# Gated attention as two streams, local attention divided at the gates, one rank for both; scan level 2 issued together with level 4

## The chip, the cores and the metric

The kernel runs on one core of one Trainium2 chip. The metric is the time of one execution in device microseconds; less is better. A core has a matrix engine (TensorE, PE in the profile), with its weight loads listed apart as PEld, a vector engine (VectorE, DVE), an activation engine (ScalarE, ACT), a general engine (GpSimd, POOL) and SyncE (SP), which here issues all DMAs. Each engine works off its own instructions in order and waits on semaphores for the others.

## What is computed

A trunk of two layers over two requests of 2048 and 512 tokens, 2560 rows of width 1024 together, in float32. The even layer projects the rows once and feeds two branches: gated linear attention (GLA, four heads, one scan in each direction with a decay that depends on the data) and local softmax attention (SWA, eight query heads over two key heads, a window of 128 to each side). Each branch is multiplied by its own gate, both go through one output projection. The odd layer is a gated convolution. A layer norm follows each.

```python
def gla_mixer(q, k, v, z, gdown, ...):
    logd_f = heads(log_sigmoid(gd_f @ w_up_f + b_f) / GLA_TAU)      # and logd_b
    o_f = _gla_scan(qh, kh, vh, logd_f, strict=False)
    o_b = flip(_gla_scan(flip(qh), flip(kh), flip(vh), flip(logd_b), strict=True))
    o = (o_f + o_b) * rsqrt(mean(square(o_f + o_b)) + NORM_EPS) * norm_g
    return o * silu(z)

def swa_mixer(q, k, v, z, rel_bias, sink):
    s = where(mask, einsum('bnqkgd,bnskd->bnkgqs', qh, kb) + bias, -inf)
    m = maximum(max(s, -1), sk)
    e = exp(s - m)
    p = e / (sum(e, -1) + exp(sk - m))
    o = einsum('bnkgqs,bnskd->bnqkgd', p, vb)
    return o * silu(z)

def trunk(x, ...):
    for l in range(DEPTH):
        sub = even_sublayer(x, ...) if l % 2 == 0 else odd_sublayer(x, ...)
        x = layer_norm(DN_ALPHA * x + sub, ln_g[l], ln_b[l])
```

## The kernel before

The rows are cut into five groups of 512 (group 4 is the short request) and twenty chunks of 128. The dense products run group by group in the order of the list `stages` in `run`: for groups 4, 3, 2, 1 the token-major part of the input projection ("tok") and the channel-major part ("ch"), then the output projection of group 4, the input projection of group 0, the odd layer's input of group 4, and so on through output projections and the odd layer, where groups are taken in pairs. Each float32 operand is split into a rounded high part and a low rest, and a product is three matrix instructions into one PSUM tile: high x high, high x low, low x high. A weight of 128 x 1024 is loaded into a raw tile `ws` (two buffers), ACT rounds it into `wh` (three buffers), and POOL subtracts to get `wl` (two buffers), in `cook` and `cook_low`; `dense_ch` then runs 16 instructions with `wh` and 8 with `wl` into an `acc` tile. The operands are `st` tiles.

Attention is threaded between these dense instructions. The order is made when the program is built: `Flow` holds generators ("side" work), `Model` keeps a clock for each engine with costs of its own, and after every dense step `pump` lets a generator continue whose inputs are due by the model's clock. Generators with a lower rank come first; the residual and operand streams have rank 0, `gla_stream` has rank 1, `swa_front` and `swa_back` rank 2. A generator that yields a list of tiles waits until the model has them written. The engines then run that order, with real semaphores. `defer` puts off a step until its tiles are due.

GLA. `gla_stream` goes through the chunks from the last to the first. For each it loads q and the decays (`gla_load`, tiles `qn`, `tA`), k in two copies (`gla_load_k`, `KK`), and runs `inside`: Q gets the decays multiplied in (`QQ`), and then seven levels s = 1, 2, 4, ..., 64 follow. A level multiplies blocks of the scaled K and Q against each other on PE (the helper `blocks`, 16 instructions of 32 x 32, which the trace lists as 32 records), then scales K and Q on DVE to the next level. For s up to 16 ACT makes a copy `km` of half of K. Level 8 is not issued at its turn: its half of Q is copied into a tile `qm` of the `md` tag, and its blocks go out together with those of level 16. Behind the levels, still in `inside`, K is transposed on PE (`turn`), the output product, the backward state `S` and the product for the forward scan are made. When a request is through, `along` carries the forward state over its chunks and makes the normed, gated output in `mix_s`.

SWA. `swa_front` takes a chunk and a key head at a time: Q·K into `ps` tiles, bias and maximum on DVE into `P`, the exponential with its sum `den` on ACT, the reciprocal, and four multiplications of `P` by it on DVE. `swa_back` transposes `P` on PE, splits it into `pth` and `ptl`, multiplies with V, and, once both key heads are there, POOL multiplies the output `o` by the gate `gb`, which goes to `mix_s`.

Tiles: PSUM has four `acc` and four `ps` tiles. In SBUF the tag `md` has eight tiles of 128 x 512, most of them for one dense output on its way to DRAM; the tag `y` has four of 128 x 1024.

Everything is issued by one helper, so that all lines of the profile read L242; groups are told apart by their tiles. DMAs are all issued by SP, one after the other.

Of the kernel before, what the change touches and what calls it, by code (L numbers as in the profile page):

```python
# [10 lines left out]
F32 = mybir.dt.float32  # L11
# [3 lines left out]
ALU = mybir.AluOpType  # L15
# [247 lines left out]
class Flow:  # L263
# [32 lines left out]
    def flush(self, everything=False, name=None):  # L296
        now, keep = [], []
        for one in self.late:
            (now if everything or name in one[2] or (name is None and one[0] <= self.t) else keep).append(one)
        self.late = self.model.late = keep  # L300
        for one in now:
            one[1]()

# [73 lines left out]
class Trunk:  # L377
    def __init__(self, tc, nc, I, y_out, ctx):
# [22 lines left out]
        self.kb_s = dr("kb_s", (2, 128, 2, T))  # L401
        self.vb_s = dr("vb_s", (NC, 128, 256))
        self.qf_s = dr("qf_s", (NC, 128, 512))
        self.up_s = dr("up_s", (128, 2, 512))
# [8 lines left out]
        self.bst = None  # L413
        self.blocks = []
        self.x, self.owned, self.refs, self.pairs, self.wblocks = {}, {}, {}, {}, {}
# [153 lines left out]
    def dense_ch(self, xh, xl, w=None, last=True):  # L569

        nc = self.nc
        wh, wl = w or self.weight()
        p = self.pd()
        for k in range(8):
            c = slice(k * 128, k * 128 + 128)
            nc.tensor.matmul(p[:], wh[:, c], xh(k), start=(k == 0), stop=False)
            nc.tensor.matmul(p[:], wh[:, c], xl(k), start=False, stop=False)
            yield
        if last:
            self.drop(wh)  # L580
            self.cook()
        for k in range(8):
            c = slice(k * 128, k * 128 + 128)
            nc.tensor.matmul(p[:], wl[:, c], xh(k), start=False, stop=(k == 7))
            if k % 2 and k < 7:
                yield
        if last:
            self.drop(wl)
        return p

# [85 lines left out]
    def setup(self):  # L676
        nc, c = self.nc, self.const
        nc.scalar.preload_act_table_set("natural_log_exp_and_others")
        load = self.load
        self.ident = load("ident", (128, 128))  # L680
        self.hl = load("hl", (128, 2))
        self.norm_g = load("norm_g", (128, 1))
        self.eps = c.tile([128, 2], F32, name="eps")
        nc.vector.memset(self.eps[:, 0:1], LN_EPS)
        nc.vector.memset(self.eps[:, 1:2], NORM_EPS)
        self.dtot = c.tile([128, NC, 4], F32, name="dtot")
        self.one = c.tile([128, 1], F32, name="one")
        nc.vector.memset(self.one[:], 1.0)
# [483 lines left out]
    def gla_load(self, c):  # L1172
# [5 lines left out]
        return q, T1  # L1178

    def gla_load_k(self, c):  # L1180
        K = self.e((128, 2, 512), "KK")
        for i in range(2):
            self.nc.sync.dma_start(K[:, i], self.k_s[c])
        return K

    def inside(self, c, first, last, ld, K, ahead):

        nc = self.nc
        q, T1 = ld
        Q = self.e((128, 2, 512), "QQ")  # L1190
        T2 = self.e((128, 2, 256), "tB")
# [28 lines left out]
        def grow_k(s):  # L1220
# [12 lines left out]
        Sb = self.bst if not last else None  # L1233
        wait = []
        for li, s in enumerate((1, 2, 4, 8, 16, 32, 64)):
            n = 512 // s
            pls = []
            if s in (8,):
                qm = self.m2(hold=True)
                nc.scalar.copy(qm[:].rearrange("p (b two s) -> p b two s", two=2, s=s), halves(Q, s))  # L1240
                wait.append((li, s, qm))
            else:
# [14 lines left out]
                for lt, t, qm in wait:  # L1257
                    km = kms.pop(t)
                    pls.append((lt, one(len(pls))))
                    blocks(pls[-1][1], lambda o: mk(km, o, [[1, 32]]), lambda o: qm[:, o:o + 32])  # L1260
                    self.drop(qm)
                wait = []
# [13 lines left out]
                else:  # L1276
                    for h in range(4):
                        for b in range(64 // s):
# [6 lines left out]
                                             tile_position=(0, hi))  # L1285
                kms.pop(s, None)
            km = None
# [12 lines left out]

            if s not in (8,):
# [6 lines left out]
            if s in (8,):  # L1308
# [6 lines left out]
            if s == 4:  # L1315
                v = self.e((128, 512), "v")
                nc.sync.dma_start(v[:], self.v_s[c])
# [5 lines left out]
        nc.vector.tensor_copy(self.dtot[:, c], mk(end, 4, [[1, 4]]))  # L1323
        ahead(0)
        self.flow.defer(lambda: nc.sync.dma_start(self.qf_s[c], Q[:, 1]), Q)

        def turn(i):
            pt = self.pw((128, 4, 128))
            for h in range(4):
                nc.tensor.transpose(pt[:, h], K[:, i, h * 128:h * 128 + 128], self.ident[:])  # L1330
            t = self.e((128, 4, 128), "km", bufs=2)
            nc.scalar.copy(t[:], pt[:])
            return t

        def grow(t):
            pv = self.pw((128, 4, 128))
            for h in range(4):
                nc.tensor.matmul(pv[:, h], t[:, h], v[:, h * 128:h * 128 + 128], start=True, stop=True)
            return pv

        kf = kb = None
        if not last:
            yield from self.bank()
            kf = turn(0)
# [3 lines left out]
                                  self.lmask16[:].rearrange("p (b s) -> p b s", s=32).unsqueeze(1).broadcast_to(wide),  # L1348
                                  acmp[:].unsqueeze(2).broadcast_to(wide))
        if not first:  # L1350
            yield from self.bank()
            kb = turn(1)
        ahead(1)
        yield [A, v] + ([Sb] if Sb is not None else [])
# [9 lines left out]
        if not first:  # L1364
# [6 lines left out]
            else:  # L1371
                for h in range(4):
                    nc.vector.scalar_tensor_tensor(Sn[:, h], Sb[:, h], mk(end, h, [[1, 1]]), pv[:, h],
                                                   op0=ALU.mult, op1=ALU.add)
            self.bst = Sn
        if not last:
# [4 lines left out]
            self.flow.defer(lambda: nc.sync.dma_start(self.m_s[c], A[:].rearrange("p h t -> p (h t)")), A)  # L1381
        yield [Q]

# [18 lines left out]
    def along(self, c, first, last, ld, ahead):  # L1402
# [13 lines left out]
        if not last:  # L1416
# [4 lines left out]
            else:  # L1421
                for h in range(4):
                    nc.vector.scalar_tensor_tensor(Sn[:, h], Sf[:, h], self.dtot[:, c, h:h + 1], m[:, h],
                                                   op0=ALU.mult, op1=ALU.add)
# [26 lines left out]
    def seq(self, g):  # L1451
        return (0, 16) if g < 4 else (16, 20)

    def gla_stream(self):
        for g in (4, 3, 2, 1, 0):
            yield "gla_in%d" % g
            c0, c1 = self.seq(g)
            ends = lambda c: (c == c0, c == c1 - 1)
            cs = list(range(4 * g + 3, 4 * g - 1, -1))
            ld, K = self.gla_load(cs[0]), self.gla_load_k(cs[0])  # L1460
            nxt = {}
            for i, c in enumerate(cs):
                yield [*ld, K]

                def ahead(n):
                    if i < 3:
                        nxt[n] = (self.gla_load, self.gla_load_k)[n](cs[i + 1])
                yield from self.inside(c, *ends(c), ld, K, ahead)
                ld, K = nxt.get(0), nxt.get(1)
            if 4 * g > c0:  # L1470
                continue
            self.bst = None
            ld = K = None
            nxt.clear()
            yield "done_e1_%d" % g
# [34 lines left out]
    def swa_front(self):  # L1510
# [16 lines left out]
        while left:  # L1527
# [10 lines left out]
            for kv in range(2):  # L1538
                while len(self.blocks) >= 2:
                    yield 1.0  # L1540
                hs = slice(4 * kv, 4 * kv + 4)
                Pt = self.e((128, 4, 385), "P", bufs=4)
                mx = self.sm((128, 4), "mx")
# [35 lines left out]
    def swa_back(self):  # L1579
# [17 lines left out]
        for n in range(40):  # L1597
# [20 lines left out]
            for kb in range(nk):  # L1618
# [14 lines left out]
                yield []  # L1633
            yield [pl, V]
            Pt = None
            self.blocks.pop(0)
# [466 lines left out]
    def run(self):  # L2103
# [101 lines left out]
```

## Time and profile before

| what | value |
|---|---|
| median of 3 runs | 2370.76 us (2369.61 to 2370.84) |
| profiled execution, its own time | 2370.12 us |
| its span, first to last instruction | 2368.1 us |
| granted PE clock, mean | 0.998 |
| DMA, mean over the span | 185 GB/s |
| PE waits, longest | 6.4 us, for the first `st` |

Busy times by engine over the span, in 40 slices (a digit is the busy share in tenths):

```profile
PE   8999999999999999999999999999999999999998
PEld 8888889888988888888888888878888877888887
DVE  2267756767767677577776467876566587656567
ACT  4666776656576645665577532543334343333431
POOL 5454435443444444444444467898887689988674
```

A row of the page gives the line, engine, operation, the tile written and the tiles read, partitions x elements and type, and the count. Then follow the busy time in us, the mean of one in ns, the idle time of the engine just before, and what ended it. PE's busy time is the union of instructions that overlap, so a 512-wide instruction is listed with some 395 ns though one starts about every 228.

### The profile page before, as it was taken

To read this page: it belongs to the slowest core of one execution; us is meant where nothing else is said; L and a number is where in the kernel's file an instruction comes from. 1 tells how busy PE (TensorE), PEld (TensorE's weight loads), DVE (VectorE), ACT (ScalarE), POOL (GpSimd) and SP (SyncE) were. 2 spreads that over 40 slices of the span, in tenths; PEclk is the share of its full clock that TensorE was granted. 3 is DMA by queue.
4 is the path that set the end of the run, shared out by engine and by line. 5 is a ranking of instruction groups with operands and counts; after the bars stand their busy time and mean duration, and the time that the engine had idled before them with its cause. 6 is when DMAs were issued, how large, how long until landed. Compare 5 with 4: busy or idle time off the path is not lost.

```text
span 2368.1 us, 43087 instructions
## 1 busy us (share of the span) xinstructions
PE 2343.9 (99%) x15830; PEld 1951.8 (82%) x15830; DVE 1582.8 (67%) x2699; ACT 1226.1 (52%) x2363; POOL 1418.4 (60%) x1610
## 2 busy tenths in 40 slices
PE   8999999999999999999999999999999999999998
PEld 8888889888988888888888888878888877888887
DVE  2267756767767677577776467876566587656567
ACT  4666776656576645665577532543334343333431
POOL 5454435443444444444444467898887689988674
PEclk9999999999999999999999999999999999999999
DMA  7977686676667657675478777232124633221573
GB/s 230 295 226 233 221 269 229 209 221 221 218 194 236 223 173 242 197 218 161 158 245 268 266 261 243 92 116 89 52 78 140 217 105 103 73 72 58 175 242 121
DMA packets 275057, 437.37 MB, mean 185 GB/s; under 512 B 21360, under 2 KB 160240, under 8 KB 274848
## 3 DMA queue, kind: packets, MB, share of 16 engines
q1 hardware_dynamic: 274848, 434.64, 56.5%
q8 instruction: 125, 2.05, 0.4%
q14 instruction: 84, 0.69, 0.1%
HBM read 319.72 MB, written 114.84 MB: 184 GB/s over the span
## 4 chain that ended last, share of the span: by engine, by line
PE 87%; DVE 5%; POOL 4%; DMA 2%; issue 1%; ACT 1%; SPq 0%; POOLq 0%; DVEq 0%; ACTq 0%
PE acc L242 71%; PE ps L242 17%; POOL wl L242 1%; POOL wh L242 1%; DVE st L242 1%; DVE bst L242 1%; DVE y L242 1%; POOL md L242 0%; SPq L242 0%; DVE QQ L242 0%; DVE P L242 0%; DVE KK L242 0%; DMA K<-kb_s 0%; DMA mix_s<-gb 0%; DMA op_s<-QQ 0%
## 5 line engine op out<-in xcount | busy, mean ns | idle before, releaser
L242 POOL TENSOR_TENSOR wl<-ws,wh 128x256 fp32r<-128x256 f32 (+1 forms) x912 | 750.7, 855 | 711.4 <-PE acc L242 478.0
L242 PE MATMUL acc<-st,wh 128*128 128x512 f32 x3160 | 828.5, 395 | 2.8 <-DVE pr L242 2.0
L242 PEld LDWEIGHTS acc<-st,wh 128*128 128x128 f32 x3160 | 580.9, 188 | 121.0 <-issue 3.1
L242 PE MATMUL acc<-st,wl 128*128 128x512 f32 x1744 | 471.9, 395 | 2.8 <-POOL wl L242 1.9
L242 PE MATMUL acc<-wh,st 128*128 128x512 f32 (+1 forms) x1680 | 389.4, 371 | 7.9 <-ACT st L242 6.4
L242 PEld LDWEIGHTS acc<-st,wl 128*128 128x128 f32 x1744 | 320.8, 188 | 68.0 <-POOL wl L242 4.1
L242 PEld LDWEIGHTS acc<-wh,st 128*128 128x128 f32 x1680 | 300.2, 189 | 55.1 <-ACT st L242 6.4
L242 ACT CAST wh<-ws 128x1024 fp32r<-128x1024 f32 (+2 forms) x252 | 249.0, 989 | 184.2 <-DMA ws<-in_w_oo 55.9
L242 PE MATMUL acc<-wl,st 128*128 128x512 f32 (+1 forms) x840 | 209.0, 368 | 0.6 <-POOL wl L242 0.5
L242 ACT ACTIVATE md<-md 128x512 f32<-128x512 f32 x264 | 164.7, 631 | 20.5 <-DVE md L242 14.9
L242 PEld LDWEIGHTS acc<-wl,st 128*128 128x128 f32 x840 | 150.7, 188 | 23.8 <-POOL wl L242 1.3
L242 DVE SCALAR_TENSOR_TENSOR md<-acc,md 128x512 f32<-128x512 f32 (+1 forms) x113 | 77.0, 683 | 81.5 <-ACT md L242 76.5
L242 DVE TENSOR_TENSOR st<-pr,st 128x512 fp32r<-128x512 f32 x115 | 98.5, 874 | 41.6 <-ACT st L242 41.2
L242 ACT ACTIVATE md<-acc 128x512 f32<-128x512 f32 (+1 forms) x133 | 76.2, 597 | 67.0 <-PE acc L242 66.5
L242 POOL TENSOR_TENSOR wh<-md,wh 128x256 fp32r<-128x256 f32 x118 | 96.7, 842 | 13.6 <-ACT wh L242 13.1
L242 ACT CAST pth<-ps 128x512 fp32r<-128x512 f32 x112 | 65.3, 583 | 73.1 <-PE ps L242 72.3
L242 DVE CUSTOM_DVE_ANT_0 P<-ps,P 128x384 f32<-128x384 f32 (+1 forms) x160 | 79.3, 525 | 29.6 <-PE ps L242 29.0
L242 ACT ACTIVATE P<-P,nm 128x385 f32<-128x385 f32 (+1 forms) x160 | 93.2, 587 | 3.9 <-DVE nm L242 3.9
L242 ACT ACTIVATE mv<-mv,eps 128x1 f32<-128x1 f32 x40 | 11.8, 295 | 151.8 <-DVE mv L242 147.7
L242 PE MATMUL acc<-P,wh 128*128 128x512 f32 x312 | 89.5, 400 | 0.4 <-POOL wh L242 0.4
L242 ACT COPY km<-KK 128x512 f32<-128x512 f32 x80 | 50.8, 635 | 72.2 <-DVE KK L242 50.9
L242 ACT CAST st<-pr 128x512 fp32r<-128x512 f32 x115 | 68.3, 617 | 30.3 <-DMA pr<-mix_s 12.9
(490 smaller groups left out, 4090.2 us busy)
## 6 DMA issues: line engine op xcount, KB each, us to landing
ws<-in_w_ch SPq DMA_DIRECT2D x105, 512.0 KB, 4.4
ws<-in_w_od SPq DMA_DIRECT2D x58, 512.0 KB, 4.2
ws<-in_w_oe SPq DMA_DIRECT2D x40, 512.0 KB, 3.8
ws<-in_w_oo SPq DMA_DIRECT2D x36, 512.0 KB, 3.5
K<-kb_s SPq DMA_DIRECT2D x32, 384.0 KB, 6.3
d_s<-md SPq DMA_DIRECT2D x40, 256.0 KB, 4.2
qb_s<-md SPq DMA_DIRECT2D x80, 128.0 KB, 3.9
tA<-d_s SPq DMA_DIRECT2D x20, 512.0 KB, 5.7
```

The costliest lines, as they stand in the source:

```text
L242: r = f(*a, **k)
```

## The change

The change has five parts.

1. Level 2 is treated like level 8: its half of Q is copied into an `md` tile, and its blocks go out with those of level 4.
2. `inside` ends after the levels. It puts what it has into a list `heads`, and a second generator, `gla_behind`, takes it from there: transposes of K, output product, state and forward product (the new function `behind`). The levels of the next chunk may run meanwhile; a counter `open` lets at most two chunks be between. Copies of K (`km`) and the transposed K (`turn`) come from the `md` tag as well, and `KK` and `QQ` may take `y` tiles.
3. `P` is no longer divided. The reciprocal is stored transposed to DRAM (`rd_s`), and read back by four DMAs a key head, each spreading one head's 128 values over 64 partitions of an `md` tile `rb`. POOL multiplies the gate by `rb`, then by the output.
4. All four attention generators have rank 1.
5. PSUM tiles of `dense_ch` are held while they are filled, and `flush` takes deferred steps off the list one at a time.

```diff
@@ class Flow
-        now, keep = [], []
...
-        self.late = self.model.late = keep
+        now = [one for one in self.late if everything or name in one[2] or (name is None and one[0] <= self.t)]
         for one in now:
-            one[1]()
+            if any(one is x for x in self.late):
+                self.late[:] = [x for x in self.late if x is not one]
+                one[1]()
@@ dense_ch
-        p = self.pd()
+        p = self.pd(hold=True)
@@ gla
+    def gla_home(self, tag):
+
+        done = self.flow.done
+        rows = "swa_in1" in done and "res_x1_4_3" not in done
+        return [(self.e2, tag, 1)] if rows or self.model.spare(tag, 1) else self.large[:1]
...
-        Q = self.e((128, 2, 512), "QQ")
+        while self.free_at(self.gla_home("QQ")) > self.flow.t:
+            yield 0.3
+        Q = self.take(self.gla_home("QQ"), (128, 2, 512))
...
+        while self.open > 1:
+            yield 0.3
+        self.open += 1
...
-                    km = kms[2 * s] = self.e((128, 512), "km", bufs=2)
+                    km = kms[2 * s] = self.take([(self.e2, "km", 2)] + self.mids, (128, 512))
...
-            if s in (8,):
+            if s in (2, 8,):
+                while self.free_at(self.mids) > self.flow.t:
+                    yield 0.3
                 qm = self.m2(hold=True)
...
-        end = tots[128]
+        nc.vector.tensor_copy(self.dtot[:, c], mk(tots[128], 0, [[1, 8]]))
+        self.heads.append((c, first, last, K, Q, base, acmp))
+        self.flow.mark("head_%d" % c)
...
+    def behind(self, c, first, last, K, Q, base, acmp, v, ahead):
...
-            t = self.e((128, 4, 128), "km", bufs=2)
+            t = self.m2((128, 4, 128), hold=True)
...
+    def gla_behind(self):
+        nxt = []
+        for c in [*range(19, 15, -1), *range(15, -1, -1)]:
+            yield "head_%d" % c
+            v = nxt.pop() if nxt else self.load_v(c)
...
+            yield from self.behind(*self.heads.pop(0), v, ahead)
@@ swa_front
-                for h in range(4):
-                    nc.vector.tensor_scalar(Pt[:, h, :w], Pt[:, h, :w], den[:, h:h + 1], None, op0=ALU.mult)
-                    if h == 1:
-                        yield []
+                nc.sync.dma_start(self.rd_s[c, kv].rearrange("h t -> t h"), den[:])
@@ swa_back
+            if kv == 0:
+                rb = self.m2(hold=True)
+            for j in range(4):
+                nc.sync.dma_start(rb[64 * kv:64 * kv + 64, 128 * j:128 * j + 128],
+                                  self.rd_s[c, kv, j:j + 1].broadcast_to([64, 128]))
...
-            yield [gb]
+            yield [gb, rb]
+            flat = gb[:].rearrange("p h t -> p (h t)")
+            nc.gpsimd.tensor_tensor(flat, flat, rb[:], op=ALU.mult)
+            self.drop(rb)
+            yield [o]
             nc.gpsimd.tensor_tensor(gb[:], o[:], gb[:], op=ALU.mult)
@@ run
         flow.add(self.gla_stream(), rank=1)
-        flow.add(self.swa_front())
-        flow.add(self.swa_back())
+        flow.add(self.gla_behind(), rank=1)
+        flow.add(self.swa_front(), rank=1)
+        flow.add(self.swa_back(), rank=1)
```

How this moves instructions shows at two places. The first is PE in the first chunk of the scan, before, from the end of level 1 to level 16 (`md` is the copied half of Q, `km` a copy of half of K, `st`, `wh` and `wl` belong to the dense work):

```order
L242 MATMUL ps<-QQ,KK 32x32 x16
L242 MATMUL acc<-st,wh 128x512 x2
L242 MATMUL acc<-st,wl 128x512 x8
L242 MATMUL acc<-st,wh 128x512 x8
L242 MATMUL ps<-QQ,km 32x32 x16
L242 MATMUL acc<-st,wh 128x512 x8
L242 MATMUL acc<-st,wl 128x512 x8
L242 MATMUL ps<-QQ,km 32x32 x16
```

The same place of the changed program:

```order
L242 MATMUL ps<-QQ,KK 32x32 x16
L242 MATMUL acc<-st,wh 128x512 x2
L242 MATMUL acc<-st,wl 128x512 x8
L242 MATMUL acc<-st,wh 128x512 x16
L242 MATMUL acc<-st,wl 128x512 x8
L242 MATMUL acc<-st,wh 128x512 x10
L242 MATMUL ps<-md,km 32x32 x16
L242 MATMUL ps<-QQ,km 32x32 x16
```

Levels 2 and 4 were two visits with 16 dense instructions between; now they are one, with 44 dense instructions between level 1 and them.

The second place is SP where the first block of local attention is handed over, in the changed program (`den` is the reciprocal, `md` the tile `rb`, `v`, `Q` and the two K tiles are inputs of the two attentions):

```order
L242 DMA rd_s<-den 128x4x1
L242 DMA V<-vb_s 128x2x256
L242 DMA gb<-gb_s 128x512
L242 DMA md<-rd_s 64x128 x4
L242 DMA v<-v_s 128x512
L242 DMA Q<-qb_s 128x1024
L242 DMA K_1732<-kb_s 128x2x384
L242 DMA K_1733<-kb_s 128x2x384
```

Before, the loads of `v`, `Q` and K stand there between weights:

```order
L242 DMA v<-v_s 128x512
L242 DMA ws<-in_w_ch 128x1024
L242 DMA Q<-qb_s 128x1024
L242 DMA K_1391<-kb_s 128x2x256
L242 DMA K_1392<-kb_s 128x2x256
```

Five DMAs have come ahead of these loads, of which the four reads need the store two rows above them to have landed.

More of the change, by code (lines that the diff above doesn't have):

```diff
@@ L1299, in grow_q @@
                 nc.vector.tensor_tensor(qq, qq, total(s, 1, n - 1), op=ALU.mult)
-            if s not in (8,):
+            if s not in (2, 8,):
                 grow_q()
@@ L1338, in grow, with place @@
                 nc.tensor.matmul(pv[:, h], t[:, h], v[:, h * 128:h * 128 + 128], start=True, stop=True)
+            self.drop(t)
             return pv
+        def place():
+            yield from self.bank()
+            while self.free_at(self.mids) > self.flow.t:
+                yield 0.3
         kf = kb = None
         if not last:
-            yield from self.bank()
+            yield from place()
             kf = turn(0)
@@ L1458, in gla_stream, with ahead @@
             ends = lambda c: (c == c0, c == c1 - 1)
[L1459 to L1462, printed above, removed]
-                yield [*ld, K]
-                def ahead(n):
-                    if i < 3:
-                        nxt[n] = (self.gla_load, self.gla_load_k)[n](cs[i + 1])
+            for c in range(4 * g + 3, 4 * g - 1, -1):
+                if 0 not in nxt:
+                    nxt[0] = self.gla_load(c)
+                while 1 not in nxt:
+                    if self.free_at(self.gla_home("KK")) <= self.flow.t:
+                        nxt[1] = self.gla_load_k(c)
+                    else:
+                        yield 0.3
+                ld, K = nxt.pop(0), nxt.pop(1)
+                yield [*ld, K]
+                def ahead(s):
+                    if c > c0 and "gla_in%d" % ((c - 1) // 4) in self.flow.done:
+                        if s == 4:
+                            nxt[0] = self.gla_load(c - 1)
+                        elif self.free_at(self.gla_home("KK")) <= self.flow.t:
+                            nxt[1] = self.gla_load_k(c - 1)
                 yield from self.inside(c, *ends(c), ld, K, ahead)
-                ld, K = nxt.get(0), nxt.get(1)
+                ld = K = None
             if 4 * g > c0:
                 continue
+            yield "tail_%d" % c0
             self.bst = None
-            ld = K = None
-            nxt.clear()
             yield "done_e1_%d" % g
```

53 lines of the change are left out of this document (33 added, 20 removed).

## The prediction

> **What bounds the kernel now.** I read the page from the top: busy times, then the chain that ended last.
>
> ```profile
> span 2368.1 us, 43087 instructions
> PE 2343.9 (99%) x15830; PEld 1951.8 (82%) x15830; DVE 1582.8 (67%) x2699; ACT 1226.1 (52%) x2363; POOL 1418.4 (60%) x1610
> ...
> PE 87%; DVE 5%; POOL 4%; DMA 2%; issue 1%; ACT 1%; SPq 0%; POOLq 0%; DVEq 0%; ACTq 0%
> ```
>
> PE is busy all but 24.2 us of the span and is 87% of the chain. What takes work from DVE, ACT or POOL therefore shortens nothing by itself; the change counts through PE, either by what its instructions take or by new waits. The order of the changed program has PE's 13,061 matrix instructions by the same shapes as before. It differs from before only up to a point: PE's last 1,365 rows are the same, and counted back in the trace they begin at about 1357 us. So I look at the stretch between the start of attention and there.
>
> ```profile
> core 0: us, PE busy (x) PEld busy (x) DVE busy (x) ACT busy (x) POOL busy (x), PEclk, DMA share, GB/s
> 120.00:1357.00 1237.00, 1235.14 (x10883) 1039.37 (x10882) 862.82 (x1803) 780.29 (x1661) 555.98 (x698) 1.00 0.69 220
> ```
>
> In 1237 us PE is idle for 1.86 us. The waits of PE in it are few and short:
>
> ```profile
> PE ps L242 <- ACT pth L242: 0.7, 1, 0.7
> PE acc L242 <- POOL wl L242: 0.5, 1, 0.5
> PE ps L242 <- DVE acmp L242: 0.2, 1, 0.2
> PE ps L242 <- DVE QQ L242: 0.2, 1, 0.2
> ```
>
> So there is no idle time to win. What is left is whether PE's busy time is all work. A busy PE is not PE at its peak, and the timeline of PE over one chunk of the scan shows where it isn't (start, length, instruction, count):
>
> ```profile
> 645.58 1.07 PE L242 MATMUL acc<-st,wh 128*128 128x512 f32 x4
> 646.58 0.46 PE L242 MATMUL ps<-QQ,km 128*32 128x32 f32 x32
> 646.97 0.73 PE L242 MATMUL acc<-st,wh 128*128 128x512 f32 x2
> 647.54 0.86 PE L242 MATMUL ps<-K,Q 128*128 128x384 f32 x4
> ...
> 650.53 0.61 PE L242 MATMUL acc<-st,wl 128*128 128x512 f32 x2
> 651.08 0.46 PE L242 MATMUL ps<-QQ,km 128*32 128x32 f32 x32
> 651.46 0.73 PE L242 MATMUL acc<-st,wl 128*128 128x512 f32 x2
> 652.03 0.60 PE L242 MATMUL ps<-ident,P 128*128 128x128 f32 x4
> ...
> 653.63 3.81 PE L242 MATMUL acc<-st,wh 128*128 128x512 f32 x16
> 657.28 1.52 PE L242 MATMUL acc<-st,wl 128*128 128x512 f32 x6
> ...
> 659.77 2.90 PE L242 MATMUL acc<-st,wh 128*128 128x512 f32 x12
> 662.60 0.46 PE L242 MATMUL ps<-md,km 128*32 128x32 f32 x32
> 662.88 0.49 PE L242 MATMUL ps<-QQ,km 128*32 128x32 f32 x32
> 663.29 1.19 PE L242 MATMUL acc<-st,wh 128*128 128x512 f32 x4
> 664.33 0.40 PE L242 MATMUL ps<-pth,V 128*128 128x512 f32 x1
> ```
>
> Levels 2 and 4 are the rows at 646.58 and 651.08; levels 8 and 16, which before already issues together, those at 662.60 and 662.88. Read starts, since lengths overlap. Sixteen dense matmuls take 657.28 - 653.63 = 3.65 us, 0.228 each. Around level 2, from 645.58 to 647.54, there are 1.96 us with six dense matmuls (1.37): the visit costs 0.59 us. Level 4: 652.03 - 650.53 = 1.50 less four dense ones (0.91), 0.59 again. The pair of levels 8 and 16: 664.33 - 659.77 = 4.56 less sixteen (3.65), 0.91 us for twice the blocks.
>
> **The change, part by part.**
>
> *Level 2 issued with level 4.* Two visits of 0.59 us become one of 0.91, with the same blocks in it: 2 x 0.59 - 0.91 = 0.27 us a chunk, and with 20 chunks **5.4 us**. In the order the separate groups of scan blocks fall from 120 to 100, so each chunk does lose one. All of it lies on PE, whose work sets the end, and nothing covers it. The price on ACT is one more copy of half of Q per chunk:
>
> ```profile
> L242 ACT COPY md<-QQ 128x512 f32<-128x512 f32 x20 | 12.4, 619 | 0.0
> ```
>
> 20 more are 12.4 us on an engine with 457 us idle in the stretch (1237.00 - 780.29), so nothing, as long as the copy is there when level 4 is.
>
> *Division moved from P to the gates.* Removed from DVE, added to POOL:
>
> ```profile
> L242 DVE TENSOR_SCALAR P<-P,den 128x384 f32<-128x384 f32 x128 | 61.6, 543 | 1.1
> ...
> L242 DVE TENSOR_SCALAR P<-P,den 128x256 f32<-128x256 f32 x32 | 10.9, 405 | 0.3
> ...
> L242 POOL TENSOR_TENSOR gb<-gb 128x512 f32<-128x512 f32 x20 | 27.3, 1367 | 61.4 <-DVE gb L242 61.4
> ```
>
> DVE loses 72.5 us of its 862.82 in the stretch, POOL gains 20 x 1.367 = 27.3 us beside 555.98. Neither is waited for by PE for more than the 0.5 us above: worth nothing, both ways. The existing multiply already waited 61.4 us for its input without PE noticing; what it holds up behind it on POOL are the low halves wl of the weights, and those are early:
>
> ```profile
> 653.80 2.84 POOL L242 TENSOR_TENSOR wl<-ws,wh 128x256 fp32r<-128x256 f32 x4 [4.37 <-PE acc L242]
> 660.53 2.83 POOL L242 TENSOR_TENSOR wl<-ws,wh 128x256 fp32r<-128x256 f32 x4 [3.90 <-ACT wh L242]
> ...
> 664.79 0.63 PE L242 MATMUL acc<-st,wl 128*128 128x512 f32 x2
> ```
>
> There are two wl buffers. PE works off the older one from 657.28; the one finished at 653.80 + 2.84 = 656.64 is first used at 664.79, 8.1 us later. Without that cover each microsecond of POOL would be one of PE.
>
> *The new transfers.* SP issues 1,505 DMAs instead of 1,304: 40 stores of the reciprocals, 160 reads that spread them over 64 partitions, and one more weight piece. An issue takes about this:
>
> ```profile
> 649.46 0.33 SPq L242 DMA_DIRECT2D ws<-in_w_ch  x1
> ...
> Q<-qb_s SPq DMA_DIRECT2D x20, 512.0 KB, 4.8
> K<-kb_s SPq DMA_DIRECT2D x32, 384.0 KB, 6.3
> v_s<-md SPq DMA_DIRECT2D x20, 168.0 KB, 2.1
> ```
>
> 201 x 0.33 = 66 us on SP, in a stretch of 1237. What counts is a wait it adds: the read waits on SP, in order, until the store before it has landed. In 6 of 40 cases it stands within four DMAs of its store (of the rest, 8 more under eight); in three of these six the loads of v, Q and K0/K1 are among those right behind it (the order of SP, shown with the change), and PE waits for them. Before shows no such transfer. Landing times bound it: nothing, where the store landed before SP came to the read, up to the 4.8 us of Q in each of the six, 29 us. Weights behind such a read have the 8 us above as cover. I also let the waits that are there now go: -1.9 us as the lower end. Between -1.9 and +29 I take +0.4, one more wait of the stretch's mean length (1.6 us in 4), since those rows are nearest: the loads of attention share SP with all weights already, and four short waits are what comes through.
>
> The Trainium skill ("DMA: Bandwidth & Descriptors", rules for kernel authors) speaks against this part: a last dim that isn't contiguous becomes one descriptor per element, and transfers under 64 KB are mostly overhead. The store, 512 single words, and the 32 KB reads are both of that kind. The page's fit of about 2 us fixed per DMA (made for the GpSimd path) would make an estimated 400 us of the 200, in flight beside PE, and no row here prices it; the sum stays as it is if they stay covered.
>
> *Two streams, one rank.* The turn, output and state steps of a chunk now run beside the levels of the next, and local attention gets the same rank. PE's instructions stay; only the neighbours change. Switching to other kinds of work is nearly free: the Q·K group at 643.95 below starts 0.92 us after four dense ones (0.91).
>
> ```profile
> 643.03 1.08 PE L242 MATMUL acc<-st,wl 128*128 128x512 f32 x4
> 643.95 0.87 PE L242 MATMUL ps<-K,Q 128*128 128x384 f32 x4
> ```
>
> I cost that at nothing. The streams hold more of the eight mid buffers ("md"), up to five at once while the dense stages want one each; cover is the three that are left.
>
> **The sum.** The profiled execution took 2370.12 us, its span 2368.1; the median shown is 2370.76, within the runs' spread. 2370.1 - 5.4 + 0.4 = **2365.1 us**.
>
> **Rivals.**
>
> 1. *The saving comes back as a wait of the pair* (no change). Level 4 now needs two copies of K and one of Q where it needed one; if PE waits 0.27 us at each of 20 pairs, 5.4 us are gone: 2370.1 - 5.4 + 5.4 = 2370.1 us. For it: the longest wait in the stretch, 0.7 us, is on a copy by ACT. Against: the pair of levels 8 and 16 has the same needs and no wait stands at its row.
>
> 2. *SP's blocked reads reach PE* (slower). Six reads, each holding the loads behind it for a full 4.8 us: 2370.1 - 5.4 + 29 = 2394 us at most. It decides from 10.8 us of waits (5.4 given back, and 5.4 from 2370.1 to 2375.5, 0.2% over the median): 1.8 us at each of the six. Waits close together can cost more than their length, as PE's timeline in a later stage and the windows around it show:
>
> ```profile
> 1549.60 0.73 PE L242 MATMUL acc<-st,wl 128*128 128x512 f32 x2 [1.14 <-POOL wl L242]
> 1551.27 1.08 PE L242 MATMUL acc<-st,wl 128*128 128x512 f32 x2 [0.94 <-DVE acc L242]
> 1552.15 4.20 PE L242 MATMUL acc<-P,wh 128*128 128x512 f32 x12
> ...
> 1550.00:1556.00 6.00, 5.07 (x16) 3.73 (x15) 4.06 (x8) 3.34 (x4) 6.00 (x8) 0.72 0.22 87
> ```
>
> After waits of 1.14 and 0.94 us the granted clock is 0.72 over six microseconds, and twelve matmuls take 4.20 us instead of some 2.9. The Trainium skill ("TensorE: Matmul & The Clock Gate", part 1) has the clock fall after an idle window of about 3.4 us; here less was enough, so the row decides. By the page waits of 1.8 us would cost their length alone. Against this rival: waits for Q or v do not appear in the stretch today.
>
> 3. *More than the visits is won*: the 1.9 us of waits go as well and some groups of blocks find a neighbour of their own kind: 2370.1 - 5.4 - 1.9 = 2362.8 us.
>
> That the change doesn't do what it says is excluded for the pairing by the count of groups.
>
> **Chances.** Forecast 0.55, rival 1 0.27, rival 3 0.10, rival 2 0.08. Differences of 0.2%, 4.7 us, are about what a measurement of this kernel can tell from no change, so faster ends at 2366.0 us. Of the forecast's 0.55 I count 0.48 below that, with rival 3 that makes faster 0.58; rival 1 and the rest of the forecast 0.34 the same; rival 2 0.08 slower. The range goes from 2360.5, some two below rival 3 because the price of a visit is read off one chunk, to 2371.5, over rival 1; it leaves out rival 2 and the edges.
>
> **What would show it.** Right: PE's timeline has level 2 and level 4 as two block rows in a row, some 0.28 us apart, with 0.9 us for the visit; PE's idle time in the stretch stays near 2 us; the identical tail starts 5 us earlier. Wrong: PE waits for ACT's copies before the pair, PE waits for v, Q or K behind reads of the reciprocals, or a granted clock below 1.00 in the stretch.

## The result and the profile after

The changed kernel takes 2554.14 us (median of 5 runs, 2550.55 to 2565.72), the kernel before 2369.7 beside it (2369.05 to 2370.84). The ratio is 1.0783, with a 95% interval of 1.0759 to 1.0806: the change makes the kernel 7.8% slower, far outside the predicted 2360.5 to 2371.5 us. Ratios here and below leave slow executions out; of the version with 20 stores these are two of four, at 2706.43 us (granted clock 0.81) and 10017.54 us.

The top of the changed kernel's page, with its busy times, two of the rows in tenths, its DMA packets and its chain:

```profile
span 2553.1 us, 43267 instructions
PE 2397.0 (94%) x15830; PEld 1990.6 (78%) x15830; DVE 1513.7 (59%) x2539; ACT 1234.2 (48%) x2384; POOL 1445.7 (57%) x1630
...
PE   8999988989799889899999899999999999999998
PEclk9999999999899989999999999999999999999999
DMA packets 309126, 442.75 MB, mean 173 GB/s; under 512 B 45057, under 2 KB 194433, under 8 KB 308913
...
PE 66%; DMA 17%; DVE 6%; POOL 3%; issue 3%; ACT 3%; SPq 2%; POOLq 0%; DVEq 0%; ACTq 0%
```

The span grew by 185.0 us. PE's idle time grew from 24.2 us to 156.1 (2553.1 - 2397.0), which is 131.9 of it, and PE's busy time by 53.1, although it executes the same 15,830 instructions. The chain, which was 87% PE and 2% DMA, now has 17% of DMA in it: transfers have become what PE waits for. The line of the packets on the page before:

```profile
DMA packets 275057, 437.37 MB, mean 185 GB/s; under 512 B 21360, under 2 KB 160240, under 8 KB 274848
```

There are 23,697 more packets under 512 B (45,057 - 21,360), and 40 stores of 512 words make 20,480 of them.

The same stretch as in the prediction, and further on, in windows of the changed kernel (columns as before: length, busy time and instructions of PE, PEld, DVE, ACT and POOL, granted clock, DMA share, GB/s):

```profile
120.00:430.00 310.00, 274.31 (x2304) 230.23 (x2304) 160.80 (x349) 183.03 (x393) 127.38 (x160) 0.95 0.77 201
430.00:860.00 430.00, 381.66 (x3674) 322.03 (x3673) 243.04 (x514) 233.36 (x453) 164.79 (x210) 0.94 0.76 186
860.00:1180.00 320.00, 293.85 (x2469) 246.47 (x2469) 178.90 (x357) 165.11 (x319) 138.56 (x168) 0.96 0.73 198
...
1700.00:2553.00 853.00, 838.70 (x3680) 685.33 (x3678) 577.92 (x707) 324.11 (x503) 689.92 (x701) 1.00 0.34 116
```

Most of the loss lies where attention runs: in the first three windows PE is idle for 35.7, 48.3 and 26.2 us at a clock of 0.94 to 0.96, where before it was idle for 1.86 us in 1237 at 1.00. Behind attention the clock is full again. The longest entries among the waits of PE (engine, tile, releaser: us in all, times, longest) show no single place:

```profile
PE ps L242 <- DMA QQ<-qf_s: 13.2, 3, 6.4
PE ps L242 <- ACT md L242: 12.6, 4, 4.6
PE ps L242 <- ACT pth L242: 12.2, 2, 8.5
...
PE ps L242 <- DMA V<-vb_s: 7.6, 3, 3.2
...
PE ps L242 <- DMA v<-v_s: 6.1, 1, 6.1
...
PE ps L242 <- DMA K<-kb_s: 4.7, 2, 3.5
```

V, v and K are among them, as the second rival had it, but also `QQ`, and engines whose own inputs came late. Among the waits of SP, which issues all DMAs, one is new and one has grown from 9.1 us, and they point to a common source:

```profile
...
SPq L242 <- DMA rd_s<-den: 105.6, 23, 9.2
...
SPq L242 <- DVE den L242: 71.7, 21, 10.2
```

SP now waits for the reciprocal to be ready, and then, in 23 cases, for its store to land. One such place is the one that the order showed with the change. SP's timeline of the changed kernel there (start and length in us, then the DMA):

```profile
161.00 0.38 SPq L242 DMA_DIRECT2D rd_s<-den  x1
161.43 0.50 SPq L242 DMA_DIRECT2D V<-vb_s  x1
161.98 0.46 SPq L242 DMA_DIRECT2D gb<-gb_s  x1
171.19 2.41 SPq L242 DMA_DIRECT2D md<-rd_s  x4
173.64 1.16 SPq L242 DMA_DIRECT2D v<-v_s  x1
```

The 2 KB store is issued at 161.00, and the reads that need it start at 171.19: SP stands from 162.44 (161.98 + 0.46) on, 8.75 us, waiting for it. That alone would leave V and the gate, issued before the wait, untouched. They aren't. The windows of the changed kernel after the store, and the rows of PE in its timeline:

```profile
164.00:172.50 8.50, 7.46 (x50) 6.99 (x47) 4.40 (x10) 7.83 (x19) 4.13 (x8) 1.00 0.23 18
172.50:176.00 3.50, 2.16 (x10) 1.43 (x14) 0.00 (x0) 0.00 (x0) 0.00 (x0) 0.76 0.51 125
...
170.68 0.78 PE L242 MATMUL acc<-wh,st 128*128 128x336 f32 x4
173.84 0.47 PE L242 MATMUL ps<-pth,V 128*128 128x512 f32 x1 [2.38 <-DMA V<-vb_s]
```

For 8.5 us all 16 DMA engines together move 18 GB/s, though V and the gate are in their queues. V, issued at 161.43, is there at about 173.8; PE waits 2.38 us for it, and the granted clock in the 3.5 us around is 0.76. So I took up a theory that is not among the prediction's rivals: **the store, cut into 512 words, holds up the transfers behind it.** Its rivals for the experiments: SP's in-order waits alone, the many small reads, the two streams with one rank, and the pairing.

### The profile page after: what moved, and what is told of

It is laid out like the page before. It is cut to its first block, busy times and chain, and to the rows that moved or that the text cites. A ratio compares the mean times of both kernels' runs of the same rounds, so it can differ in the third digit from the quotient of the medians.

```text
span 2553.1 us, 43267 instructions
## 1 busy us (share of the span) xinstructions
PE 2397.0 (94%) x15830; PEld 1990.6 (78%) x15830; DVE 1513.7 (59%) x2539; ACT 1234.2 (48%) x2384; POOL 1445.7 (57%) x1630
## 2 busy tenths in 40 slices
DMA packets 309126, 442.75 MB, mean 173 GB/s; under 512 B 45057, under 2 KB 194433, under 8 KB 308913
## 4 chain that ended last, share of the span: by engine, by line
PE 66%; DMA 17%; DVE 6%; POOL 3%; issue 3%; ACT 3%; SPq 2%; POOLq 0%; DVEq 0%; ACTq 0%
PE acc L242 55%; PE ps L242 11%; DMA V<-vb_s 2%; SPq L242 2%; POOL wl L242 2%; DMA ws<-in_w_ch 2%; DMA rd_s<-den 2%; DVE st L242 1%; ACT md L242 1%; DMA pr<-in_xT 1%; DMA ws<-in_w_od 1%; DVE y L242 1%; DMA pr<-x_s 1%; DMA pr<-mix_s 1%; DMA tA<-qf_s 1%
## 5 line engine op out<-in xcount | busy, mean ns | idle before, releaser
L242 PE MATMUL acc<-st,wh 128*128 128x512 f32 x3096 | 816.8, 399 | 11.5 <-ACT wh L242 7.7
L242 PE MATMUL acc<-st,wl 128*128 128x512 f32 x1712 | 465.2, 398 | 3.0 <-POOL wl L242 2.9
L242 DVE TENSOR_TENSOR ptl<-ps,pth 128x512 fp32r<-128x512 f32 x112 | 76.4, 682 | 51.3 <-ACT pth L242 51.2
L242 DVE TENSOR_TENSOR y<-y,tC 128x512 f32<-128x512 f32 (+1 forms) x61 | 44.1, 744 | 94.5 <-PE ps L242 70.3
L242 PE MATMUL ps<-K,Q 128*128 128x384 f32 (+1 forms) x320 | 75.4, 350 | 24.7 <-ACT A L242 8.1
```

What stands on the lines that cost most here:

```text
L242: r = f(*a, **k)
```

## The experiments

"Whole change" is the changed kernel. Ratios are to the kernel before, on the same chip, with their 95% intervals; a ratio step of 0.001 is 2.4 us.

**The change without the division at the gates.** `P` is divided on DVE as before; streams, ranks and pairing stay.

```diff
-                nc.sync.dma_start(self.rd_s[c, kv].rearrange("h t -> t h"), den[:])
+                for h in range(4):
+                    nc.vector.tensor_scalar(Pt[:, h, :w], Pt[:, h, :w], den[:, h:h + 1], None, op0=ALU.mult)
...
-                nc.sync.dma_start(rb[64 * kv:64 * kv + 64, 128 * j:128 * j + 128],
-                                  self.rd_s[c, kv, j:j + 1].broadcast_to([64, 128]))
...
-            nc.gpsimd.tensor_tensor(flat, flat, rb[:], op=ALU.mult)
```

> The changed kernel with the division put back on P (four multiplications on DVE a block, no store of the reciprocals, no reads of them, no second POOL multiplication); streams, ranks and the pairing of levels 2 and 4 stay. If the stores of single words plug the DMA queues, or if SP's waits for den and for the landing of the store hold up what is behind them: 2360 to 2368 us, all of the loss gone. If the two streams, their hold on md tiles or the pairing make the waits: 2500 us or more.

Measured: 2373.52 us, ratio 1.0015 (1.0006 to 1.0023). Its busy times and the prediction's stretch:

```profile
PE 2338.6 (99%) x15830; PEld 1952.7 (82%) x15830; DVE 1576.7 (66%) x2699; ACT 1236.0 (52%) x2384; POOL 1416.3 (60%) x1610
...
120.00:1357.00 1237.00, 1226.27 (x10867) 1037.79 (x10867) 858.47 (x1804) 787.21 (x1669) 552.41 (x699) 1.00 0.69 221
```

182 of the 186 us are gone. PE's busy time is 5.3 us less than before (2343.9 - 2338.6), but in the stretch PE is now idle for 10.7 us instead of 1.9. Streams, ranks and pairing together cost some 4 us; the loss is in the division at the gates.

**The division at the gates alone**, in the kernel before: the reverse of that edit, no streams, no new ranks, no pairing.

> The kernel of before with only the division moved to the gates. If the division is the cause, by the words or by SP's order: 100 to 190 us slower than before, 2470 to 2560 us, with SP's waits for rd_s and den as in the changed kernel. If streams or pairing are the cause: within 5 us of before.

Measured: 2604.44 us, ratio 1.0985 (1.0965 to 1.1005). That is more than the whole change costs. SP's waits in it:

```profile
SPq L242 <- DVE den L242: 113.7, 24, 12.0
SPq L242 <- DMA rd_s<-den: 108.9, 24, 10.5
```

The part is slower by itself, and with the rest of the change around it it costs less. Why it costs less there isn't shown. Which of its operations is slow stays open here too: store, reads or the second multiplication on POOL.

**The word store alone, dead.** On the first experiment (`P` divided), each reciprocal is also stored as in the whole change. Nothing reads it.

```diff
+                nc.sync.dma_start(self.rd_s[c, kv].rearrange("h t -> t h"), den[:])
                 for h in range(4):
```

> The division on P as in e1, and the 40 stores of den as single words left in as dead work; no reads. If the stores themselves plug the DMA queues: most of the loss is back, 2450 to 2550 us, and the loads right behind a store land about 10 us late. If SP's wait for the landing of the store, at the reads, is the cause: that wait is gone, 2360 to 2390 us.

Measured: 2503.73 us, ratio 1.0563 (1.0545 to 1.0580). Forty stores of 2 KB that nobody reads cost (1.0563 - 1.0015) x 2369.7 = 130 us, 3.2 us each.

**The same 2 KB as 128 rows of 16 bytes.** The dead store writes `den` in its own layout, four values a row. Bytes, place, queue and SP's wait for `den` stay.

```diff
-    self.rd_s[c, kv].rearrange("h t -> t h")
+    self.rd_s[c, kv].rearrange("a b -> (a b)").rearrange("(t h) -> t h", h=4)
```

> As e5, with the dead store of den laid out so that each partition's four words are one row of 16 bytes: the same 2 KB, issued at the same place with the same wait of SP for den, 128 pieces instead of 512. If the number of single words plugs the queues: a quarter of the loss or less, 2375 to 2410 us. If SP's wait for den (99 us in e5) is the cause: about 2500 us, as e5.

Measured: 2375.6 us, ratio 1.0023 (1.0012 to 1.0035). SP's waits for `den`, first of the kernel with words, then of that with rows:

```profile
SPq L242 <- DVE den L242: 99.3, 31, 9.6
```

```profile
SPq L242 <- DVE den L242: 102.3, 29, 9.8
```

The waits are equal, and the loss of 130 us has gone. So SP's standing for `den` costs next to nothing, and the form of the store is what costs. Three things change with it at once: 128 pieces for 512, 16 bytes each for 4, and a straight order in DRAM for a transposed one. No run tells these three apart. The nine microseconds behind the first store show what the form does. In the kernel with words (issued at 159.44):

```profile
161.00:170.00 9.00, 6.41 (x96) 5.69 (x95) 4.87 (x14) 3.45 (x7) 2.08 (x4) 0.93 0.17 30
```

In the kernel with rows (issued at 160.33):

```profile
162.00:171.00 9.00, 7.93 (x110) 7.12 (x109) 8.54 (x21) 6.63 (x14) 3.37 (x7) 1.00 0.82 269
```

30 GB/s against 269, for the same bytes and the same loads behind. `V` lands 4.5 us after its issue behind the rows; behind the words of the whole change it took 12.4 (161.43 to 173.8). DVE and ACT are about half as busy beside it. The words themselves are soon through: in the kernel with words 528 packets under 512 B start between 160 and 161 us, 512 words and 16 more, then 99 packets of 512 B and more up to 162, and from 162.5 to 164 no packet starts at all. So the traffic doesn't stand because words fill the whole time; what holds it after them the traces don't show.

**Word stores for one key head only**, 20 instead of 40, as a dose.

```diff
+                if kv == 0:
                     nc.sync.dma_start(self.rd_s[c, kv].rearrange("h t -> t h"), den[:])
```

> As e5 (dead stores of single words, no reads), with the store for one of the two key heads only, 20 instead of 40. If each store holds up the queues by itself: half of the 130 us between e1 and e5, 2425 to 2455 us. If it takes two close together to do harm: 2375 to 2410 us.

Measured: 2439.91 and 2447.04 us, ratio 1.0308 (1.0279 to 1.0338), over the first experiment (1.0308 - 1.0015) x 2369.7 = 69 us, 0.53 of the 130. Half the stores, half the loss.

**The word store deferred** until the planner has `den` due, so that SP stands less.

```diff
-                nc.sync.dma_start(...)
+                self.flow.defer(lambda ...: nc.sync.dma_start(...), den)
```

> As e5, with the dead store of single words put off until den is due by the planner's clock, so that SP should come to it when den is there. If SP's wait for den is the cause: 2370 to 2400 us. If the words plug the queues: within 25 us of e5, 2480 to 2530 us.

Measured: 2478.87 us, ratio 1.0461 (1.0447 to 1.0476). SP's wait for `den` falls to a third of what it was, and 24 of the 130 us go with it:

```profile
SPq L242 <- DVE den L242: 33.1, 18, 5.9
```

Behind the first store the rate is still only 43 GB/s (161.50 to 170.50). Fewer waits or other neighbours of the store: the run doesn't tell which. The row store, with its 102 us of that wait and no loss, speaks against the waits alone.

**The word store on ACT's queue** instead of SP's.

```diff
-                nc.sync.dma_start(self.rd_s[c, kv].rearrange("h t -> t h"), den[:])
+                nc.scalar.dma_start(self.rd_s[c, kv].rearrange("h t -> t h"), den[:])
```

> As e5, with the dead stores of single words issued by ACT, whose queue is another than SP's. If the words hold up only what is behind them in the queue that issued them: 2375 to 2400 us. If they hold up the DMA engines for every queue: 2470 to 2530 us, as e5.

Measured: 2495.82 us, ratio 1.0525 (1.0505 to 1.0546), 9 us less than the 1.0563 from SP, so that most of the loss stays. Here the first store is issued at 160.43, and SP's loads are in another queue:

```profile
162.00:171.00 9.00, 5.37 (x91) 4.83 (x90) 4.82 (x13) 3.45 (x7) 2.09 (x4) 0.92 0.86 38
```

They come to 38 GB/s all the same. Among them are the loads of `Q` and K, which SP issues at 164.01 and 164.38, when the 528 packets of ACT's queue (162 to 163 us) are through. The words therefore hold up more than the queue that they stand in, and also transfers that are issued after them. What they hold inside the chip isn't shown: the DMA engines are listed as busy for 0.86 of this window and for 0.17 of the one above.

**The reads alone.** The first experiment with the 160 reads, from a constant array instead of the reciprocals; what they read is not used.

```diff
+                nc.sync.dma_start(rb[64 * kv:64 * kv + 64, 128 * j:128 * j + 128],
+                                  self.I["ident"][j:j + 1].broadcast_to([64, 128]))
```

> As e1 (division on P), with the 160 reads of 512-byte rows spread over 64 partitions left in, taken from an array that stands in DRAM from the start, so that they wait for no store; nothing uses what they bring. If the reads cost something by themselves (issue time on SP, DMA traffic, one more md tile): 2378 to 2390 us, which with the words would make up the whole loss. If only the words and the wait for their landing cost: 2371 to 2376 us, as e1.

Measured: 2367.36 us, ratio 0.9991 (0.9981 to 1.0001). The reads cost nothing. The planner orders the program a little differently with them, and that alone seems to be worth the 0.0024 to the first experiment; smaller differences between two planned orders shouldn't be put down to an edit.

**The whole change with the reciprocals turned by PE.** `den` is transposed to four rows of 128 values, and the store is four rows of 512 bytes; reads and both multiplications on POOL stay. 40 transposes and 40 small ACT copies are added.

```diff
-                nc.sync.dma_start(self.rd_s[c, kv].rearrange("h t -> t h"), den[:])
+                yield [den]
+                yield from self.bank()
+                dp = self.pw()
+                nc.tensor.transpose(dp[:4, :128], den[:], self.ident[:])
+                dn = self.m2((4, 128))
+                nc.scalar.copy(dn[:], dp[:4, :128])
+                yield [dn]
+                nc.sync.dma_start(self.rd_s[c, kv], dn[:])
```

> The changed kernel complete, but den is turned by PE (128 x 4 to 4 x 128) and copied by ACT, so that the store is four rows of 512 bytes; the reads and both POOL multiplications stay. If the single words are the cause: 2375 to 2410 us, with SP's wait for the landing of the store at 2 to 5 us instead of 9. If any store that is read back does it, by SP's order: 2500 us or more.

Measured: 2382.69 us, ratio 1.0061 (1.0044 to 1.0077): 171 of the 186 us ((1.0783 - 1.0061) x 2369.7) leave with the words. The first store is issued at 163.66 and the reads that need it start at 166.46, after 2.80 us instead of 10.19. SP still waits for stores to land, but briefly:

```profile
SPq L242 <- DMA rd_s<-md: 22.7, 15, 3.8
```

The three `yield`s let the planner put the store later, where its data are due, so that SP no longer stands for `den` either. Form and place change together here; that the form alone does it rests on the row store.

**The pairing alone**, in the kernel before, `(8,)` to `(2, 8)` at its three places.

> The kernel of before with only level 2 issued together with level 4. If a visit costs 0.59 us and a pair 0.91: 20 x 0.27 = 5.4 us less, 2363 to 2366 us. If PE waits for the copies instead: 2369 to 2371 us.

Measured: 2406.39 us, ratio 1.0150 (1.0136 to 1.0163). Neither theory had this. Its windows show where it is lost:

```profile
120.00:1300.00 1180.00, 1178.86 (x10591) 995.85 (x10590) 822.79 (x1716) 742.30 (x1492) 547.90 (x675) 1.00 0.67 211
1300.00:1545.00 245.00, 216.73 (x990) 177.20 (x989) 156.49 (x231) 104.81 (x286) 128.45 (x142) 0.91 0.73 243
```

Up to 1300 us PE is idle for 1.1 us in 1180, as before (1.86 in 1237). Then it is idle for 28 in 245, where before 240 us from 1300 held 1.4. The largest waits of PE there:

```profile
PE ps L242 <- DVE md L242: 11.6, 3, 7.3
PE ps L242 <- ACT km L242: 6.1, 2, 3.5
```

The pair costs PE nothing at its place. The scan, however, ends later. Its last outputs are stored to `mix_s` from `qn` tiles; the last of these stores is issued at 1358.4 us before (first line) and at 1436.9 with the pair (second line; at the end of each stand the first and the last start):

```profile
L242 SPq DMA_DIRECT2D mix_s<-qn x10: 524/525/847, 334.1 to 1358.4; - x10
L242 SPq DMA_DIRECT2D mix_s<-qn x10: 518/519/561, 370.2 to 1436.9; - x10
```

In the first experiment, which has the same pairs in two streams, it is 1362.6, and the loss is gone. So the single stream gets through its chunks more slowly with the pair, and the last stages, which need the end of attention, wait. That this is because level 4 has to wait for both copies is argued, and not shown by a run of its own.

**The streams without the pairing**, the first experiment with `(2, 8,)` back to `(8,)`.

> As e1 (division on P), with level 2 issued at its own turn again, so that the two streams, the ranks and the homes of tiles are what is left of the change. If a pair saves 0.27 us on PE here too: 5 us above e1, 2377 to 2381 us. If the pairing is given back as waits: 2372 to 2375 us, as e1.

Measured: 2376.56 us, ratio 1.0030 (1.0019 to 1.0042), PE busy 2342.3 us, 3.7 more than with the pairing. The times point to the same 3.6 us, but the intervals touch and the planned orders differ, so that the worth of pairing within the streams isn't settled by these two.

**A higher price for scan blocks in the planner.** On the first experiment, the model's cost of a block of 32 columns goes from 0.02 to 0.03, so that a chunk of the scan takes longer by its clock.

```diff
-            return (0.02 if n <= 32 else n / 600 + 0.011), 0.25
+            return (0.03 if n <= 32 else n / 600 + 0.011), 0.25
```

> As e1, with the planner's price of a 32-column block raised from 0.02 to 0.03 us, which is nearer to the 0.028 of a pair and the 0.037 of a single visit that the trace shows, so that its clock is nearer to PE's. Nothing else is changed, but the order comes out anew. If the waits that e1 has over before come from the planner's clock running ahead of PE: 2363 to 2369 us, faster than before. If not: 2370 to 2378 us.

Measured: 2365.0 us, ratio 0.9982 (0.9973 to 0.9992). Its busy times, and one pair of levels 2 and 4 in PE's timeline:

```profile
PE 2335.9 (99%) x15830; PEld 1952.2 (83%) x15830; DVE 1572.2 (67%) x2699; ACT 1236.9 (52%) x2384; POOL 1420.3 (60%) x1610
...
625.32 1.07 PE L242 MATMUL acc<-wl,st 128*128 128x336 f32 x6
626.32 0.46 PE L242 MATMUL ps<-md,km 128*32 128x32 f32 x32
626.59 0.49 PE L242 MATMUL ps<-QQ,km 128*32 128x32 f32 x32
627.01 0.57 PE L242 MATMUL acc<-wl,st 128*128 128x336 f32 x2
627.43 0.78 PE L242 MATMUL acc<-wh,st 128*128 128x336 f32 x4
628.04 0.47 PE L242 MATMUL acc<-wl,st 128*128 128x336 f32 x2
```

This version is a little faster than both kernels. It has the streams, the rank and the pairs, and divides `P` as before; its 0.18% lies close to what can be told apart.

**What the runs add up to**, in us of the 2369.7:

| part | from | us |
|---|---|---|
| streams, one rank, pairing | 1.0015 - 1 | 3.6 |
| 40 word stores, dead | 1.0563 - 1.0015 | 129.9 |
| the store read back, division at the gates | 1.0783 - 1.0563 | 52.1 |
| whole change | 1.0783 - 1 | 185.6 |

The third row is a difference. SP's 105.6 us of standing for stores to land belong to it; with the four rows of 512 bytes most of it goes too, since only 14.5 us ((1.0061 - 1) x 2369.7) of the whole change are left then.

## Why the prediction was wrong

**The step that failed is "the new transfers".** The prediction put them at +0.4 us, between -1.9 and +29. In its place the runs showed some 171 us that leave with the words (the version with four rows, where the store also comes later), and 130 us from the word stores alone. Three things went wrong in that step:

- *The nearest row wasn't near.* The landing of Q, 4.8 us for 512 KB in long rows, was taken as the upper end for a 2 KB store, as if fewer bytes could only be faster. The trace of before has no store in single words, so nothing bounded this one. It takes some 10 us (161.00 to 171.19).
- *Only the reads close behind their store were counted*, 6 of 40, those that could hold up SP. With stores that take some 10 us SP stood for a landing 23 times. And all 40 stores cost, 3.2 us each without any read, because they hold up transfers that are already in the queues or come shortly after. The prediction asked who waits for the store, not what moves beside it.
- *The rule of the Trainium skill was named and then given no price.* "DMA: Bandwidth & Descriptors" (rules for kernel authors) makes one descriptor of each element of a last dim that isn't contiguous; the trace agrees, with 23,697 more packets under 512 B. The prediction went on with "the sum stays as it is if they stay covered". They weren't, and it was the rule on the store that mattered here. The other rule quoted, that transfers under 64 KB are mostly overhead, is about the 32 KB reads as well, and those cost this kernel nothing (0.9991).

**The second rival had the sign and the place, not the mechanism.** Loads of V, v and K came late behind the reciprocals, as it said, and the granted clock fell. But it let SP's standing do this, at six places, for 24 us net at most, and the prediction gave it a chance of 0.08. SP's waits for `den` are worth nothing by themselves (the row store), and those for the landing belong to the smaller of the two large rows of the table.

**Waits cost more than their length**, as the row in the prediction had it: PE idles 131.9 us more, and takes 53.1 us longer for the same work. The Trainium skill ("TensorE: Matmul & The Clock Gate", part 1) lets the clock fall after some 3.4 us without work; here, behind a wait of 2.38 us, the granted clock is 0.59 from 173.80 to 177.00, so that the measurement decides again.

**Level 2 with level 4: the size was right, the place not free.** In the timeline of the version with the higher block price the two rows start 0.27 us apart (626.32 and 626.59), as forecast. From 625.32 to 627.43 there are 2.11 us with eight dense matmuls, of 0.153 each by the next four (627.43 to 628.04); that leaves 0.89 us for the visit, where 0.91 was forecast. PE's busy time fell by 5.3 us in the first experiment (forecast 5.4), though by 3.7 against the streams without pairs. What the prediction missed is that with the pair the scan ends later: in the single stream that goes with a loss of 1.5%, which sits at the stages' ends, some 650 us behind the rows that were read. Rival 1 looked for it as a wait at the pair.

**The streams are not free either.** PE's idle time in the stretch went from 1.9 to 10.7 us in the first experiment; that eats the 5.3 us and leaves +3.6. The prediction had them at nothing because switching between kinds of work is nearly free, which says nothing of waits.

**The 72.5 us taken from DVE won nothing**, as predicted: the version with rows has DVE at 1522.0 us of its span instead of 1582.8 and is still slower than before. That POOL's added 27.3 us cost nothing isn't shown as sharply: between that version and the first experiment lie 10.9 us ((1.0061 - 1.0015) x 2369.7), in which they stand together with 40 transposes and the waits for the stores.

## What to carry to other kernels

Price a DMA by its pieces before its bytes, and then ask what is in flight beside it: a 2 KB store in words cost 3 to 4 us of the kernel because the loads behind it nearly stood still. When the trace of before has nothing like a new transfer, its price is unknown and not small, and the change should be tried with the same bytes in rows. A change that lengthens a chain with a due date shows its price where that chain ends, so read the ends of the stages as well as the place of the edit.

## What the runs showed of the hardware

- A DRAM store of 512 four-byte words in transposed order keeps the DMA engines from moving much of anything else for about 9 us: 18, 30, 38 and 43 GB/s in four kernels behind their first store, where 128 rows of 16 bytes in straight order leave 269. Issued on ACT's queue instead of SP's it costs little less (1.0525 against 1.0563). Number, size and order of the pieces were not told apart.
- The DMA share doesn't show this: 0.23 and 0.17 in two of these windows, 0.86 in a third, at rates of 18, 30 and 38 GB/s. GB/s does.
- One wait of 2.38 us was enough to lower the granted clock: 1.00 from 164.00 to 172.50, 0.59 from 173.80 to 177.00. Over the 430 us from 430 to 860, with PE busy for 89%, it was 0.94; single waits of 7.5, 7.7 and 8.5 us are among those in there.
